# Attention weights turned on TensorE one block at a time, with another product between two of them

## The chip, the cores and the metric

The kernel runs on one core of a Trainium2 chip. The metric is the device time of one execution in microseconds (us), from the median of several runs. The engines of the core are TensorE (PE in the profile, and PEld for its loads of stationary operands), VectorE (DVE), ScalarE (ACT), GpSimd (POOL) and SyncE (SP, which issues most DMAs). Each takes its own instructions in the order in which the program wrote them.

## The reference

Two layers, each over 512 tokens of width 1024 in float32. Cut to what matters here:

```python
def hybrid_layer(x, w_in, w_out, ln_g, ln_b, rel_bias, topk):
    proj = jnp.einsum('bsd,dn->bsn', x, w_in)
    qA, kA, vA, gA, qB, kB, vB, gB, qI, kI, wI = jnp.split(proj, SPLIT_POINTS, axis=-1)
    oA = stick_breaking_attention(...)      # 8 heads of 64
    oB = dsa_sparse_attention(...)          # 8 heads of 64, top 128 keys of each query
    mix = jnp.concatenate([oA * jax.nn.silu(gA), oB * jax.nn.silu(gB)], axis=-1)
    y = jnp.einsum('bsm,md->bsd', mix, w_out)
    return layer_norm(ALPHA * x + y, ln_g, ln_b)
```

In the first group a weight is `sigmoid(z)` times the product of `1 - sigmoid` over the keys between it and the query. In the second group an indexer scores all keys, the best 128 of each query take part in a soft-max with a bias by distance, and the others are masked.

## The kernel before, in words

Every float32 operand of a product is held as a high and a low part (`XH` and `XL`, `whi` and `wlo`), and a product is three matmuls: high by high, low by high, high by low. A layer is a fixed list of 88 tasks. 24 are blocks of the indexer, then come 32 `Stick` tasks (8 heads of 4 blocks of 128 queries; block `qb` sees the first `qb + 1` blocks of keys), then 32 `Soft` tasks of the same shape. The loop over `s` in `layer` is the pipeline: in slot `s`, task `s` gets its logits `z` on PE (`stage0`: two matmuls of 128 to 512 columns), older tasks go through their later stages, and PE's remaining time in the slot is filled with matmuls of the big projections.

A `Soft` block goes like this. In slot `s` PE writes `z` (L518, L523); DVE subtracts the bias and finds the row's extreme (L762); ACT takes the exponential into `p` (L767). In the next slot, for the last head of a layer alone, ACT also scales `p` by the reciprocal of its sum (L777). In slot `s + 2` PE turns `p` around, block by block of 128 x 128 (`transpose`, L530, `qb + 1` transposes into the PSUM tile `tr`); ACT copies all of `tr` to the tile `AT` as its high part, one instruction (`evacuate`, L538), and DVE makes the low part from `tr` and the high part (`evacuate_lo`, L541). In slot `s + 3`, behind the last block of a head, PE multiplies `AT` with the values into `o`: eight matmuls at L701, the first with the high part, the second and third with the low part (`steps = [(1, 1), (2, 1), (1, 0), ...]`, where the second number is 1 for low). A `Stick` block runs the same way (transposes in slot `s + 3`, L727 and L730 in place of L538 and L541). Where a `Stick` head ends while a new one begins, the eight value matmuls are woven: one behind each of the first two `z` matmuls of 128 columns, the rest behind the transposes.

The fills are generators (`project_t`, `project_v`, `out_project`) that stand in one queue in a hand-written order; one step of a generator issues three matmuls (L266 to L268 of 512 columns into `pj`, L303 to L305 of 256 columns into `pjv`, L809 of 512 columns into `pjo`). `fill(t)` takes steps until the cost of the steps taken reaches the target at time `t` of a table of pins, and a slot calls it up to three times: ahead of the transposes, behind the low evacuation, and at its end. ACT, DVE and POOL take their instructions in the order of this loop: on ACT, for one, the evacuation of the older block stands ahead of the exponential of the new one (`stage1b`).

In the last four slots of a layer no `z` is left: PE has transposes of the last three blocks, six fill matmuls behind each run of transposes, the eight value matmuls of the last head, and then the output projection with nothing between (`pjo`, 90 matmuls in a row in the first layer, 162 in the second, by the chain of waits).

Of the kernel before, what the change touches and what calls it, by code (L numbers as in the profile page):

```python
# [17 lines left out]
P = 128  # L18
# [3 lines left out]
KC = D // P  # L22
# [80 lines left out]
def tile_hybrid(ctx: ExitStack, tc: tile.TileContext, xt, x, w_in, w_ki, w_out, ln_g, ln_b, rel_bias, onehot, out, depth=DEPTH):  # L103
# [154 lines left out]
    def run(gen):  # L258
# [2 lines left out]
            stream.prep_ahead()  # L261
        flush()

    def mm3(o, w, kc, first, last, tb):
        o = o.rearrange("p (a b) -> p a b", b=P)[:, tb:]
        T.matmul(o, w[0], XH[:, tb:, kc, :], start=first, stop=False)  # L266
        T.matmul(o, w[0], XL[:, tb:, kc, :], start=False, stop=False)  # L267
        T.matmul(o, w[1], XH[:, tb:, kc, :], start=False, stop=last)  # L268

    def first_block(unit):  # L270
        return 1 if unit[0] == "I" else 0
# [14 lines left out]
    def project_v(l, unit, vt, keys=None):  # L286
        i = index[l, unit]
        if keys is None:
            stream.prep(i + 1)
            w = [[t.rearrange("p (a b) -> p a b", b=W256) for t in stream.done[i + h]] for h in range(2)]  # L290
        else:
            stream.prep(i + 2)
            w = joined
        n = w[0][0].shape[2]
        vv = vt.rearrange("p t (h r) -> p t h r", r=P)
        for tb in range(NTB):
            if tb:
                stream.want = i + min(tb + 1, 3) + (keys is not None)
            full = ppj.tile([P, S], F32, tag="pj", name="pjv")[:, :n]
            acc = full[:, :W256]  # L300
            for kc in range(KC):
                whi, wlo = (t[:, kc % 4, :] for t in w[kc // 4])
                T.matmul(full, XH[:, tb, kc, :], whi, start=kc == 0, stop=False)  # L303
                T.matmul(full, XL[:, tb, kc, :], whi, start=False, stop=False)  # L304
                T.matmul(full, XH[:, tb, kc, :], wlo, start=False, stop=kc == KC - 1)  # L305
                if kc == KC - 1:
                    if keys is not None:
                        later.append(lambda tb=tb, full=full: keep_keys(tb, full))
                    if unit[0] == "A":
                        later.append(lambda tb=tb, acc=acc: A.activation(V_NOW[:, tb, :], acc, AF.Copy))  # L310
                    else:
                        later.append(lambda tb=tb, acc=acc: evac_v(vv, tb, acc))
                if (tb, kc) == (NTB - 1, KC - 1) and unit[0] == "A":
                    later.append(shift_values)
                    pending.append([SHIFT_SLOTS[1], lambda: value_steps(vv)])
                yield 324 * n // W256
# [193 lines left out]
    class Block:  # L510
# [13 lines left out]
            for head in weave:  # L524
                head.value(*head.steps.pop(0))

        def transpose(self):
            self.tr = ptr.tile([P, S], F32, tag="tr", name="tr")
            for sb in range(self.qb + 1):
                T.transpose(self.tr[:, sb * P : (sb + 1) * P], self.p[:, sb * P : (sb + 1) * P], ident)  # L530

        def blocks(self, t):
            b = t[:, self.qb * P : self.qb * P + P]
# [24 lines left out]
    def layer(l):  # L558
        last_layer = l == depth - 1
        st = {}  # L560
# [237 lines left out]
        def out_project(half, mts, tb, evac, acc=None, cols=slice(0, S), by_kind=False):  # L798
            if acc is None:
                acc = ppj.tile([P, S], F32, tag="pj", name="pjo")  # L800
            kinds = ((XH, 0), (XL, 0), (XH, 1))
            steps = [(m, k) for m in range(2 * mts[0], 2 * mts[-1] + 2) for k in kinds]
            if by_kind:
                early, all_ = range(2 * mts[0], 2 * mts[-1]), range(2 * mts[0], 2 * mts[-1] + 2)
                steps = [(m, k) for k, ms in ((0, early), (2, early), (0, all_[-2:]), (1, all_), (2, all_[-2:])) for m in ms]
                steps = [(m, kinds[k]) for m, k in steps]
            for n, (m, (mixed, part)) in enumerate(steps):
                w = stream.done[index[l, "o"] + 4 * half + m // 2][part][:, m % 2 * S : (m % 2 + 1) * S]
                T.matmul(acc[:, cols], mixed[:, tb, m, :], w[:, cols], start=n == 0, stop=n == len(steps) - 1)  # L809
                if n == len(steps) - 1:  # L810
                    later.append(lambda: evac(acc))
                if n % 3 == 2:
                    yield 648
# [13 lines left out]
        def target(s):  # L827
            for (a, ca), (b, cb) in zip(pins, pins[1:]):
                if s <= b:
                    return ca + (cb - ca) * max(0.0, (s - a) / max(b - a, 1e-9))  # L830
            return total

        st["done"] = 0
        st["gen"] = None

        def fill(s):
            while st["done"] < target(s) - 300:
                if st["gen"] is None:
                    if not queue:
                        return  # L840
                    st["gen"] = queue.pop(0)()
                step = next(st["gen"], None)
                if step is None:
                    st["gen"] = None
                else:
                    st["done"] += step

        rounds = [qb for _ in range(TOPK // 8) for qb in range(1, NTB)]

# [49 lines left out]
        for s in range(SLOTS + 3):  # L899
# [34 lines left out]
            if not sticks[0]:  # L934
                fill(now + FRAC[0])
            for old in olds:
                old.transpose()
                old.evacuate(old.head.at)
            if ended[0]:
                done.head.rest_of_values()  # L940
# [213 lines left out]
```

## Time and profile before

| what | value |
|---|---|
| median of 3 runs | 633.24 us (632.79 to 633.54) |
| the profiled execution's own time | 633.23 us |
| its span, first to last instruction | 631.4 us |
| PE busy | 622.5 us (99%), 3501 matmuls |
| DVE, ACT, POOL busy | 494.7, 343.6, 366.4 us |
| mean granted TensorE clock | 0.996 of full |
| transposes at L530 | 320: 160 of `om` (Stick), 160 of `p` (Soft) |

A matmul's record begins when PE starts to read for it and lasts until its result has landed, so neighbours overlap and a busy PE says little. What a matmul costs PE is the distance from its start to the next one's start. In a row of the time line, a row with "xN" holds N matmuls of one group that follow each other, and its duration runs from the first's start to the last's end. A number in front of a row is its start in us from the start of the span.

### The profile page before, as it was taken

The page shows a single profiled execution, that of the slowest core. Times are in us where ns is not written, and L with a number is a line of the kernel's source. Part 1 is how long each engine was busy: PE and PEld are TensorE (multiplying, and loading weights), DVE is VectorE, ACT ScalarE, POOL GpSimd, SP SyncE. Part 2 cuts the span into 40 slices and gives each one's busy share as a digit, 9 for nine tenths or more (in the row PEclk, how much of TensorE's full clock was granted, in tenths as well). Part 3 has the DMA queues.
Part 4 walks back from the last instruction along what each step waited for, and adds up shares of the span by engine and source line. Part 5 has one row for each costly group of instructions (what it writes and reads, how often), then busy time and mean ns, then how long its engine had stood idle before and what let it go on. Part 6 is the DMA issues. An engine that isn't in the chain of part 4 may idle for free.

```text
span 631.4 us, 10261 instructions
## 1 busy us (share of the span) xinstructions
PE 622.5 (99%) x3501; PEld 542.7 (86%) x3501; DVE 494.7 (78%) x1058; ACT 343.6 (54%) x686; POOL 366.4 (58%) x380
## 2 busy tenths in 40 slices
PE   9999999999999999999999999999999999999995
PEld 7988888988889889878899888899888898898784
DVE  3878999999975775668845789999999667656676
ACT  5686545454447566883135855554535566678700
POOL 5563544468465776898134544525756577778721
PEclk9999999999999999999999999999999999999998
DMA  7624243222362475453314242323123725644402
GB/s 239 215 78 133 101 133 102 82 86 68 98 174 80 133 187 168 124 191 118 134 68 133 103 133 100 114 87 125 43 101 90 194 86 140 171 131 142 166 34 100
DMA packets 31779, 77.41 MB, mean 123 GB/s; under 512 B 6572, under 2 KB 10668, under 8 KB 31728
## 3 DMA queue, kind: packets, MB, share of 16 engines
q1 hardware_dynamic: 31440, 76.51, 39.1%
q8 instruction: 27, 0.44, 0.3%
q10 hardware_dynamic: 288, 0.26, 0.1%
q14 instruction: 24, 0.20, 0.1%
HBM read 61.84 MB, written 4.44 MB: 105 GB/s over the span
## 4 chain that ended last, share of the span: by engine, by line
PE 91%; ACT 3%; POOL 2%; DMA 1%; DVE 1%; issue 1%; DVEq 0%; SPq 0%; POOLq 0%; ACTq 0%
PE pj L266 15%; PE pj L268 15%; PE pj L267 15%; PE pjo L809 11%; PE o L701 5%; PE tr L530 5%; PE z L523 4%; PE pjv L303 4%; PE pjv L304 4%; PE pjv L305 4%; PE z L518 4%; PE pjv L428 2%; PE pjq L430 1%; POOL wlo L215 1%; ACT p L767 1%; ACT p L777 1%
## 5 line engine op out<-in xcount | busy, mean ns | idle before, releaser
L215 POOL TENSOR_TENSOR wlo<-raw,whi 128x256 fp32r<-128x256 f32 (+1 forms) x250 | 230.9, 954 | 142.1 <-ACT whi L212 141.2
L266 PE MATMUL pj<-XH,whi 128*128 128x512 f32 (+1 forms) x432 | 171.6, 397 | 0.0
L268 PE MATMUL pj<-XH,wlo 128*128 128x512 f32 (+1 forms) x432 | 166.4, 385 | 0.0
L267 PE MATMUL pj<-XL,whi 128*128 128x512 f32 (+1 forms) x432 | 166.1, 385 | 0.0
L268 PEld LDWEIGHTS pj<-XH,wlo 128*128 128x128 f32 x432 | 81.1, 188 | 16.1
L266 PEld LDWEIGHTS pj<-XH,whi 128*128 128x128 f32 x432 | 81.2, 188 | 13.1
L717 ACT ACTIVATE om<-z 128x128 f32<-128x128 f32 (+1 forms) x64 | 28.1, 438 | 118.1 <-issue 68.4
L267 PEld LDWEIGHTS pj<-XL,whi 128*128 128x128 f32 x432 | 81.4, 188 | 12.4
L212 ACT ACTIVATE whi<-raw 128x1024 fp32r<-128x1024 f32 x78 | 82.0, 1056 | 2.5 <-DMA raw<-in_w_in_dram 1.9
L722 DVE TENSOR_TENSOR_SCAN om<-om,future 128x128 f32<-128x128 f32 (+1 forms) x64 | 67.6, 1056 | 0.2
L603 POOL TENSOR_TENSOR M<-M,mixt 64x512 f32<-64x512 f32 x24 | 33.9, 1413 | 51.0 <-DVE mixt L602 36.0
L303 PE MATMUL pjv<-whi,XH 128*128 128x256 f32 x192 | 56.8, 296 | 0.0
L305 PE MATMUL pjv<-wlo,XH 128*128 128x256 f32 x192 | 54.3, 283 | 0.0
L304 PE MATMUL pjv<-whi,XL 128*128 128x256 f32 x192 | 54.2, 282 | 0.0
L854 DVE MAX8 m<-scores 128x8 f32<-128x256 f32 (+2 forms) x96 | 52.9, 551 | 0.1
L855 DVE MATCH_REPLACE8 scores<-m,scores 128x256 f32<-128x256 f32 (+2 forms) x96 | 52.1, 543 | 0.0
L767 ACT ACTIVATE p<-p,mn 128x128 f32<-128x128 f32 (+1 forms) x64 | 35.8, 560 | 23.9 <-DVE mn L762 23.5
L701 PE MATMUL o<-AT,vt 128*128 128x512 f32 (+7 forms) x256 | 48.6, 316 | 0.0
L809 PE MATMUL pjo<-whi,XH 128*128 128x512 f32 (+1 forms) x118 | 41.2, 387 | 0.0
L809 PE MATMUL pjo<-wlo,XH 128*128 128x512 f32 (+1 forms) x118 | 41.0, 383 | 0.0
L523 PE MATMUL z<-k,q 128*128 128x128 f32 (+3 forms) x128 | 40.9, 320 | 0.0
L541 DVE TENSOR_TENSOR AT<-tr,AT 128x128 fp32r<-128x128 f32 (+1 forms) x64 | 31.2, 488 | 11.7 <-ACT AT L538 11.3
(165 smaller groups left out, 1290.8 us busy)
## 6 DMA issues: line engine op xcount, KB each, us to landing
raw<-in_w_in_dram SPq DMA_DIRECT2D x66, 512.0 KB, 3.4
k<-k SPq DMA_DIRECT2D x32, 256.0 KB, 5.1
raw<-in_w_out_dram SPq DMA_DIRECT2D x14, 512.0 KB, 3.2
gbias<-f_dram SPq DMA_DIRECT2D x18, 256.0 KB, 3.9
XN<-in_x_dram SPq DMA_DIRECT2D x8, 256.0 KB
y_dram<-XN SPq DMA_DIRECT2D x4, 512.0 KB, 2.6
XN<-y_dram SPq DMA_DIRECT2D x8, 256.0 KB, 3.9
M<-M SPq DMA_DIRECT2D x4, 448.0 KB
```

The lines of the kernel that those rows point to most:

```text
L212: A.activation(hi, src, AF.Copy)
L215: low = lambda lo=lo[:, c], src=src[:, c], hi=hi[:, c]: lo_engine.tensor_tensor(lo, src, hi, ALU.subtract)
L266: T.matmul(o, w[0], XH[:, tb:, kc, :], start=first, stop=False)
L267: T.matmul(o, w[0], XL[:, tb:, kc, :], start=False, stop=False)
L268: T.matmul(o, w[1], XH[:, tb:, kc, :], start=False, stop=last)
L303: T.matmul(full, XH[:, tb, kc, :], whi, start=kc == 0, stop=False)
L304: T.matmul(full, XL[:, tb, kc, :], whi, start=False, stop=False)
L305: T.matmul(full, XH[:, tb, kc, :], wlo, start=False, stop=kc == KC - 1)
L523: T.matmul(self.z[:, :nn], c, d, start=False, stop=True)
L701: T.matmul(self.o[:m, sb * P :], vt[:, sb, self.hh * P : self.hh * P + m], at_block(self.at[j], sb, sb, NTB - sb), start=(sb, j) == (0, 0) ...
L722: V.tensor_tensor_scan(rev, rev, future[:, S - n :][:, ::-1], 1.0, ALU.mult, ALU.max)
L809: T.matmul(acc[:, cols], mixed[:, tb, m, :], w[:, cols], start=n == 0, stop=n == len(steps) - 1)
```

## The change

`transpose` becomes `transposes`, which returns the single transposes as functions. In the slot loop the first of them is issued as before. For a `Soft` block the others go to a list, and steps of the fill queue are taken there and then; each fill matmul is issued through `fill_matmul`, which issues one waiting transpose behind it. So one fill matmul stands between two transposes. The steps count as done, and the later `fill` calls of the slot take as many fewer. For a `Stick` block whose slot also holds woven value matmuls, one value matmul goes between its two transposes; the other `Stick` blocks keep their transposes in one run. The evacuation is written behind the last transpose, as before.

```diff
+    between_fills = []
+
+    def fill_matmul(*args, **flags):
+        T.matmul(*args, **flags)
+        if between_fills:
+            between_fills.pop(0)()
...
-        T.matmul(o, w[0], XH[:, tb:, kc, :], start=first, stop=False)
+        fill_matmul(o, w[0], XH[:, tb:, kc, :], start=first, stop=False)
...
-        def transpose(self):
+        def transposes(self):
             self.tr = ptr.tile([P, S], F32, tag="tr", name="tr")
-            for sb in range(self.qb + 1):
-                T.transpose(self.tr[:, sb * P : (sb + 1) * P], self.p[:, sb * P : (sb + 1) * P], ident)
+            c = [slice(sb * P, (sb + 1) * P) for sb in range(self.qb + 1)]
+            return [lambda c=c: T.transpose(self.tr[:, c], self.p[:, c], ident) for c in c]
...
+        def next_fill():
+            if st["gen"] is None:
+                if not queue:
+                    return False
+                st["gen"] = queue.pop(0)()
+            step = next(st["gen"], None)
+            if step is None:
+                st["gen"] = None
+            else:
+                st["done"] += step
+            return True
+
         def fill(s):
-            while st["done"] < target(s) - 300:
...
+            while st["done"] < target(s) - 300 and next_fill():
+                pass
...
             for old in olds:
-                old.transpose()
+                first, *others = old.transposes()
+                first()
+                if old is softs[0]:
+                    between_fills.extend(others)
+                    while between_fills and next_fill():
+                        pass
+                    while between_fills:
+                        between_fills.pop(0)()
+                for t in others if old is sticks[0] else ():
+                    if ended[0]:
+                        done.head.value(*done.head.steps.pop(0))
+                    t()
                 old.evacuate(old.head.at)
```

The other fill matmuls (of `project_v` and `out_project`) go through `fill_matmul` in the same way. The instructions of ACT, DVE, POOL and SP stand in the same order before and after; only PE's order changes, and each slot holds the same matmuls as before. 110 of the 320 transposes get a matmul ahead of them in place of a transpose: 48 of `p` in each layer (18 behind 256-column fills, 30 behind 512-column ones) and 7 of `om` in each layer.

Three places show it. The first is on PE near the end of the first layer, in the slot that turns the last block (`qb` 3) of the last head but one: `z` is the newest block's logits, `tr<-ident,p` the transposes, `pjo` the fills of the output projection. Before:

```order
L518 MATMUL z<-k,q 128x256
L523 MATMUL z<-k,q 128x256
L530 MATMUL tr<-ident,p 128x128 x4
L809 MATMUL pjo<-whi_3012,XH 128x512
L809 MATMUL pjo<-whi_2815,XL 128x512 x2
L809 MATMUL pjo<-whi_2891,XL 128x512 x2
L809 MATMUL pjo<-whi_3012,XL 128x512
L518 MATMUL z<-k,q 128x384
```

And now:

```order
L525 MATMUL z<-k,q 128x256
L530 MATMUL z<-k,q 128x256
L537 MATMUL tr<-ident,p 128x128
L267 MATMUL pjo<-whi_3012,XH 128x512
L537 MATMUL tr<-ident,p 128x128
L267 MATMUL pjo<-whi_2815,XL 128x512
L537 MATMUL tr<-ident,p 128x128
L267 MATMUL pjo<-whi_2815,XL 128x512
L537 MATMUL tr<-ident,p 128x128
L267 MATMUL pjo<-whi_2891,XL 128x512 x2
L267 MATMUL pjo<-whi_3012,XL 128x512
L525 MATMUL z<-k,q 128x384
```

The first transpose stands where it stood; the fourth has moved behind three fill matmuls that used to follow it.

The second place is PE at the end of the layer, where the last block of the last head is turned and its values follow (`o<-AT_107` reads the high part, `o<-AT_108` the low part). Before:

```order
L809 MATMUL pjo<-whi_2815,XL 128x512 x2
L530 MATMUL tr<-ident,p 128x128 x4
L809 MATMUL pjo<-whi_2891,XL 128x512 x2
L809 MATMUL pjo<-whi_3012,XL 128x512 x2
L809 MATMUL pjo<-wlo_3013,XH 128x512 x2
L701 MATMUL o<-AT_107,vt 128x512
L701 MATMUL o<-AT_108,vt 64x384
```

And now:

```order
L267 MATMUL pjo<-whi_2815,XL 128x512 x2
L537 MATMUL tr<-ident,p 128x128
L267 MATMUL pjo<-whi_2891,XL 128x512
L537 MATMUL tr<-ident,p 128x128
L267 MATMUL pjo<-whi_2891,XL 128x512
L537 MATMUL tr<-ident,p 128x128
L267 MATMUL pjo<-whi_3012,XL 128x512
L537 MATMUL tr<-ident,p 128x128
L267 MATMUL pjo<-whi_3012,XL 128x512
L267 MATMUL pjo<-wlo_3013,XH 128x512 x2
L708 MATMUL o<-AT_107,vt 128x512
L708 MATMUL o<-AT_108,vt 64x384
```

Between the last transpose and the first value matmul stood six fill matmuls; now three stand there.

The third place is a woven `Stick` run on PE in the first layer (`tr<-ident,om`). Before:

```order
L523 MATMUL z<-k,q 128x128
L701 MATMUL o<-AT_106,vt 64x256
L530 MATMUL tr<-ident,om 128x128 x2
L701 MATMUL o<-AT_105,vt 128x384
L701 MATMUL o<-AT_105,vt 128x256
```

And now:

```order
L530 MATMUL z<-k,q 128x128
L708 MATMUL o<-AT_106,vt 64x256
L537 MATMUL tr<-ident,om 128x128
L708 MATMUL o<-AT_105,vt 128x384
L537 MATMUL tr<-ident,om 128x128
L708 MATMUL o<-AT_105,vt 128x256
```

The second transpose has moved behind the value matmul of 384 columns.

More of the change, by code (lines that the diff above doesn't have):

```diff
@@ L262, in run @@
         flush()
+    between_fills = []
[3 more added lines that the diff above has]
+            between_fills.pop(0)()
     def mm3(o, w, kc, first, last, tb):
         o = o.rearrange("p (a b) -> p a b", b=P)[:, tb:]
-        T.matmul(o, w[0], XH[:, tb:, kc, :], start=first, stop=False)
-        T.matmul(o, w[0], XL[:, tb:, kc, :], start=False, stop=False)
-        T.matmul(o, w[1], XH[:, tb:, kc, :], start=False, stop=last)
+        fill_matmul(o, w[0], XH[:, tb:, kc, :], start=first, stop=False)
+        fill_matmul(o, w[0], XL[:, tb:, kc, :], start=False, stop=False)
+        fill_matmul(o, w[1], XH[:, tb:, kc, :], start=False, stop=last)
     def first_block(unit):
@@ L302, in project_v @@
                 whi, wlo = (t[:, kc % 4, :] for t in w[kc // 4])
-                T.matmul(full, XH[:, tb, kc, :], whi, start=kc == 0, stop=False)
-                T.matmul(full, XL[:, tb, kc, :], whi, start=False, stop=False)
-                T.matmul(full, XH[:, tb, kc, :], wlo, start=False, stop=kc == KC - 1)
+                fill_matmul(full, XH[:, tb, kc, :], whi, start=kc == 0, stop=False)
+                fill_matmul(full, XL[:, tb, kc, :], whi, start=False, stop=False)
+                fill_matmul(full, XH[:, tb, kc, :], wlo, start=False, stop=kc == KC - 1)
                 if kc == KC - 1:
@@ L808, in out_project @@
                 w = stream.done[index[l, "o"] + 4 * half + m // 2][part][:, m % 2 * S : (m % 2 + 1) * S]
-                T.matmul(acc[:, cols], mixed[:, tb, m, :], w[:, cols], start=n == 0, stop=n == len(steps) - 1)
+                fill_matmul(acc[:, cols], mixed[:, tb, m, :], w[:, cols], start=n == 0, stop=n == len(steps) - 1)
                 if n == len(steps) - 1:
@@ L834, in layer @@
         st["gen"] = None
-        def fill(s):
-            while st["done"] < target(s) - 300:
[L838 to L846, printed above, removed]
+        def next_fill():
[9 more added lines that the diff above has]
+            return True
+        def fill(s):
+            while st["done"] < target(s) - 300 and next_fill():
+                pass
         rounds = [qb for _ in range(TOPK // 8) for qb in range(1, NTB)]
```

## The prediction

> **What bounds the kernel now.** The page comes first: the span, PE's share of it, and the chain of work that ended last.
>
> ```profile
> span 631.4 us, 10261 instructions
> ...
> PE 91%; ACT 3%; POOL 2%; DMA 1%; DVE 1%; issue 1%; DVEq 0%; SPq 0%; POOLq 0%; ACTq 0%
> ```
>
> PE is the bound over nine tenths of the span. So a nanosecond per transpose on PE counts in full there, and the rest is decided by where PE waits. The waits of PE's loads say that it hardly does in the attention part:
>
> ```profile
> PEld tr L530 <- ACT p L777: 1.5, 4, 0.6
> ...
> PEld o L701 <- DVE AT L541: 1.0, 4, 0.3
> ```
>
> Columns: total us, times, longest. Four times a transpose waits for the scaled `p` of a layer's last head, four times a value matmul waits for the low part of `AT`. The chain, asked for its end of the first layer, shows what leads to the first of these (start, us, what):
>
> ```profile
> 270.86 0.50 ACT p L767 x2
> 271.36 0.48 ACT AT L538
> 271.84 0.29 ACT p L777
> 272.13 0.49 ACT p L767 x2
> ...
> 277.99 0.73 ACT p L777
> 278.73 0.04 issue
> 278.77 0.66 PE tr L530 x4
> 279.43 1.38 PE pjo L809 x6
> 280.81 1.18 PE o L701 x8
> ```
>
> And the window view has ACT's busy time (fourth engine) in the 7.4 us between, here and at the same place of the second layer:
>
> ```profile
> 271.30:278.70 7.40, 7.40 (x39) 5.61 (x37) 4.59 (x16) 7.12 (x18) 6.45 (x6) 1.00 0.56 178
> 581.80:589.20 7.40, 7.37 (x39) 5.47 (x37) 4.62 (x16) 7.12 (x18) 6.37 (x6) 1.00 0.55 186
> ```
>
> ACT works 7.12 of 7.40 us, in program order, from an `AT` evacuation to the `p` that the last run of transposes waits for. From there to the end of the layer PE has no idle time (the last three rows of the chain, then 90 output matmuls). So at two places per layer something that ACT or DVE does late makes PE late, and the change moves work towards both.
>
> **The price of a transpose on PE.** Two stretches of PE's time line, among 512-column fills, first a run of four, then a transpose that stands singly already before the change (blocks with `qb` 0 have one):
>
> ```profile
> 221.31 0.39 PE L268 MATMUL pj<-XH,wlo 128*128 128x512 f32 x1
> 221.54 0.60 PE L530 MATMUL tr<-ident,p 128*128 128x128 f32 x4
> 221.90 0.48 PE L266 MATMUL pj<-XH,whi 128*128 128x512 f32 x1
> 222.21 0.40 PE L267 MATMUL pj<-XL,whi 128*128 128x512 f32 x1
> ...
> 225.11 0.27 PE L530 MATMUL tr<-ident,p 128*128 128x128 f32 x1
> 225.14 0.47 PE L266 MATMUL pj<-XH,whi 128*128 128x512 f32 x1
> 225.45 0.39 PE L267 MATMUL pj<-XL,whi 128*128 128x512 f32 x1
> ```
>
> A 512-column matmul holds PE for 0.23 us (221.31 to 221.54). The run, with the one fill behind it, takes 222.21 - 221.54 = 0.67 us; less the fill's 0.23 that is 0.44 for four, 0.11 each. The single transpose with its fill takes 225.45 - 225.11 = 0.34 us, less 0.23: 0.11 again. The fill behind a transpose starts 0.03 after it but then runs 0.08 longer (0.47 against 0.39), so nothing is hidden; it is only booked elsewhere. The single one is exactly what the change makes of the others: a 512-column fill, a transpose, a 512-column fill. The same among 256-column fills:
>
> ```profile
> 246.02 0.60 PE L530 MATMUL tr<-ident,p 128*128 128x128 f32 x4
> 246.37 0.36 PE L303 MATMUL pjv<-whi,XH 128*128 128x256 f32 x1
> 246.57 0.28 PE L304 MATMUL pjv<-whi,XL 128*128 128x256 f32 x1
> 246.69 0.28 PE L305 MATMUL pjv<-wlo,XH 128*128 128x256 f32 x1
> ...
> 248.24 0.27 PE L530 MATMUL tr<-ident,p 128*128 128x128 f32 x1
> 248.27 0.36 PE L303 MATMUL pjv<-whi,XH 128*128 128x256 f32 x1
> 248.47 0.28 PE L304 MATMUL pjv<-whi,XL 128*128 128x256 f32 x1
> ```
>
> Here a fill is 0.12 (246.57 to 246.69). Four in a run: 0.55 - 0.12 = 0.43, 0.11 each. One alone: 0.23 - 0.12 = 0.11. For the 110 transposes that the change separates PE pays the same, within what two decimals can show: between 0 and 0.01 us more each, 0 to 1.1 us in all. I take 0.3, near the lower end, since the rows agree. The 14 woven `Stick` transposes are among the 110; the value matmul that goes between has the same load of 128 columns behind a transpose as the fills have, so I price it alike.
>
> The Trainium skill, in "TensorE: Matmul & The Clock Gate", section "LDWEIGHTS (loading the stationary operand)", gives a load of 128 columns about 128 / 1.2 = 107 ns, and in "Part 2: What happens when you issue a matmul" it says that a load is pulled ahead under the matmul that is running. By that a run of transposes goes at the pace of loads, which the trace bears out (0.11 each), and a transpose between two wide fills has its own load hidden, which speaks for this change. But by the same rule the next fill's load then has only the transpose to hide under, and comes into the open instead; the row at 225.11 (0.11 us for a lone transpose) agrees with that second half.
>
> **What comes later.** ACT's evacuation of `tr` waits for the last transpose of its run. In a run the fourth starts 0.33 us after the first (221.90 - 0.03 - 221.54). With fills between, each step is 0.34 (225.11 to 225.45), so it starts 1.02 after: 0.69 us later, while the first stands where it did. Among 256-column fills the step is 0.23 and the shift 0.36. For most of the 48 slots per kernel with such runs this costs nothing: the `AT` blocks are read a slot later, and the new block's exponential, behind the evacuation on ACT, is needed two slots later, each slot being 2 to 4 us. `p`, `tr` and `z` have room for that: PE shows no wait there now. I price these at zero; at the worst a slip of one `p` by 0.24 us (a run of three among 256-column fills, 2 x (0.23 - 0.11)) runs through POOL's weight splits into PE in the first layer.
>
> Two places per layer have no such cover. The first is the evacuation of the last block of the last head but one. PE's run and ACT's instruction, in the first and the second layer:
>
> ```profile
> 270.42 0.60 PE L530 MATMUL tr<-ident,p 128*128 128x128 f32 x4
> 271.27 0.57 ACT L538 ACTIVATE AT<-tr 128x512 fp32r<-128x512 f32 x1
> ...
> 580.81 0.60 PE L530 MATMUL tr<-ident,p 128*128 128x128 f32 x4
> 581.79 0.58 ACT L538 ACTIVATE AT<-tr 128x512 fp32r<-128x512 f32 x1
> ```
>
> Before, the run ends at 271.02 and the evacuation starts at 271.27, behind an exponential. After, it ends at 271.02 + 0.69 = 271.71 and the evacuation starts 0.04 later (by the row at 279.46 below, 0.03 after the run's end at 279.43): at 271.75, 0.48 later. From here ACT is full, so the scaled `p` that the last run waits for at 278.77 comes 0.48 later too. PE's fills in this stretch can't help: PE waits there already. In the second layer the same gives 580.81 + 0.60 + 0.69 + 0.04 = 582.14 against 581.79: 0.35. Together **0.83 us**; the bounds are 0, if ACT has slack that its rows hide (7.40 - 7.12 = 0.28 per layer is the most that shows), and 0.48 in each.
>
> The second place is the last run of all, with its evacuation, its low part on DVE and the values:
>
> ```profile
> 279.46 0.60 ACT L538 ACTIVATE AT<-tr 128x512 fp32r<-128x512 f32 x1 [0.37 <-PE tr L530]
> ...
> 280.10 0.69 DVE L541 TENSOR_TENSOR AT<-tr,AT 128x512 fp32r<-128x512 f32 x1 [0.41 <-ACT AT L538]
> ...
> 280.65 1.34 PE L701 MATMUL o<-AT,vt 128*128 128x512 f32 x8
> ...
> 590.62 0.69 DVE L541 TENSOR_TENSOR AT<-tr,AT 128x512 fp32r<-128x512 f32 x1 [0.41 <-ACT AT L538]
> ...
> 591.17 1.35 PE L701 MATMUL o<-AT,vt 128*128 128x512 f32 x8
> ```
>
> Before, the run begins at 278.77 and ends at 279.43; ACT is done at 280.06, DVE at 280.79. PE reaches the first value matmul at 280.65 and the second, which reads the low part, at 280.88: 0.09 to spare. After, the run ends 0.69 later, so DVE is done at 281.48. PE, whose six fills and four transposes are the same, still reaches the second value matmul at 280.88 and now waits; with the 0.05 that its load needs behind the wait, it starts at 281.53, 0.65 later. Queued behind it are the other six value matmuls and the whole output projection, and nothing on PE takes it up. The second layer ends the same way (the low part done at 591.31, the second value matmul at 591.40: the same 0.09). Together **1.30 us**; the bounds are 0 and 2 x 0.75.
>
> The sum: 0.3 + 0.83 + 1.30 = 2.4 us on the profiled execution's 633.23, whose span is 631.4 and which agrees with the median, 633.24. That makes **635.7 us**, 0.4% slower. About 0.2% (1.27 us) is what a measurement of this kernel can tell from no change.
>
> **The rivals.** *Faster: the loads are hidden after all.* The mechanism is the first half of the rule cited above: alone between wide fills a transpose costs only its streaming. The nearest row is a 128-column matmul in the woven part:
>
> ```profile
> 111.49 0.22 PE L518 MATMUL z<-k,q 128*128 128x128 f32 x1
> 111.55 0.34 PE L701 MATMUL o<-AT,vt 128*64 128x384 f32 x1
> ```
>
> It holds PE for 0.06 us, so 0.05 less than a transpose. 110 x 0.05 = 5.5 us saved, less up to the 2.1 us of the two late places: 629.8. It decides as soon as a lone transpose costs under 0.09 us. Against it stand the lone transposes in the trace, at 0.11 among both kinds of fill, and that the matmul at 111.55 has a stationary operand of 64 columns, which the fills have not. I give it 0.08.
>
> *No change: the late evacuations are covered.* ACT makes up the 0.83 in gaps or in an order of events that the profile hides, or the values find their low part in time. With one of the two gone the time is 634.4 or 634.8, with both 633.5. Against it: DVE's 0.69 and ACT's 0.60 are in series with the run, and ACT's gaps in the window are 0.28. For a result within 0.2% I give 0.20.
>
> *Slower still.* The lone transposes cost the full 0.01 more each (+0.8 over what I took), and the 0.24 us slip of the first layer arrives: 636.7 to 637.0. It is inside the forecast's side; I count it with it, at 0.72 in all.
>
> *The change does nothing* can be left out: the order shows no run of `p` transposes left.
>
> **How the numbers follow.** The likeliest is the forecast, 635.7. The range goes down through the covered cases to 633.3 (only the 0 to 0.3 us on PE) and up to 637.0 (all upper bounds); left out are the faster rival's 0.08 and a tenth for what I have not seen. Faster by over 0.2%: 0.08; within: 0.20; slower by over 0.2%: 0.72.
>
> **What would show it.** Right: a transpose with the fill behind it still takes 0.34 us among 512-column fills and 0.23 among 256-column ones; the evacuation that now starts at 271.27 starts about 0.5 us later against the run's first transpose, and the last run with it; the second value matmul of a layer's last head starts about 0.9 us after the first, in place of 0.23, and PE's loads at L701 wait for DVE some 1.3 us more in total. Wrong: a transpose and its fill in 0.30 us or less, a stretch between 200 and 255 us that is shorter than before, or a last run of transposes that begins no later than before.

## The result, and the profile after

The kernel with the change takes 637.19 us (median of 6 executions, 636.82 to 637.60); the kernel before takes 633.39 us (6 executions, 632.79 to 634.21). The ratio is 1.0057, with a 95% interval of 1.0048 to 1.0067: 3.8 us slower. The direction was forecast, the size was not: 635.7 was the number and 637.0 the end of the range.

The page of the changed kernel, its span and the chain of waits:

```profile
span 635.5 us, 10261 instructions
...
PE 94%; ACT 3%; DVE 1%; DMA 1%; issue 0%; SPq 0%; POOL 0%; DVEq 0%; POOLq 0%; ACTq 0%
```

PE carries even more of the chain than before (94% against 91%). That doesn't say that PE has more work. The waits of its loads (total us, times, longest) say that it waits longer:

```profile
PEld tr L537 <- ACT p L784: 2.3, 4, 0.6
PEld o L708 <- DVE AT L548: 1.7, 4, 0.5
...
PEld tr L537 <- ACT p L774: 0.9, 2, 0.5
PEld o L708 <- ACT AT L545: 0.9, 2, 0.4
```

L537, L784, L708 and L548 are the former L530, L777, L701 and L541; L774 and L545 are the former L767 and L538. The first wait was 1.5 us and the second 1.0 us before. The third was 0.5, with 0.2 at the longest; the fourth is new among the ten longest. The prediction had asked for some 1.3 us more of the second wait. It is 0.7 more, because the fourth now stands ahead of it: the first value matmul already waits, for ACT's high part.

The single transposes, on PE's time line, among 512-column fills and among 256-column fills:

```profile
222.53 0.27 PE L537 MATMUL tr<-ident,p 128*128 128x128 f32 x1
222.56 0.48 PE L267 MATMUL pj<-XL,whi 128*128 128x512 f32 x1
222.88 0.27 PE L537 MATMUL tr<-ident,p 128*128 128x128 f32 x1
...
246.97 0.27 PE L537 MATMUL tr<-ident,p 128*128 128x128 f32 x1
247.00 0.37 PE L267 MATMUL pjv<-whi,XL 128*128 128x256 f32 x1
247.20 0.27 PE L537 MATMUL tr<-ident,p 128*128 128x128 f32 x1
```

From transpose to transpose it is 0.35 and 0.23 us with one fill between: 0.34 and 0.23 had been forecast. To within 0.01 us the separated transposes of `p` cost what they cost in a run.

Next the two late places. ACT's evacuation of the last block of the last head but one, and ACT's busy time (fourth engine) from there to the end of the scaled `p` that the last run needs, in both layers:

```profile
272.85 0.60 ACT L545 ACTIVATE AT<-tr 128x512 fp32r<-128x512 f32 x1 [0.51 <-PE tr L537]
...
585.14 0.60 ACT L545 ACTIVATE AT<-tr 128x512 fp32r<-128x512 f32 x1 [0.46 <-PE tr L537]
```

```profile
272.88:280.32 7.44, 7.21 (x37) 5.10 (x35) 4.12 (x13) 7.16 (x17) 5.94 (x6) 1.00 0.57 196
585.17:592.60 7.43, 7.21 (x37) 5.09 (x35) 4.12 (x13) 7.15 (x17) 5.92 (x6) 1.00 0.64 195
```

ACT now waits for PE's transposes 0.51 and 0.46 us, where it came behind an exponential before. Then it is as full as it was: 7.16 of 7.44 us, against 7.12 of 7.40 before. And the end of the layer:

```profile
280.37 0.33 PE L537 MATMUL tr<-ident,p 128*128 128x128 f32 x1
...
282.43 0.50 PE L708 MATMUL o<-AT,vt 128*128 128x512 f32 x1
283.15 1.16 PE L708 MATMUL o<-AT,vt 128*64 128x384 f32 x7 [0.23 <-DVE AT L548]
```

The second value matmul starts 0.72 us after the first, in place of 0.23 (280.65 to 280.88 before). The first one is late as well: ACT's copy was done 0.59 us before PE came to it (280.06 and 280.65 before), and the run, counted from its own start, now ends 0.71 later (280.37 to 281.74, against 278.77 to 279.43).

Set against the profiled execution of before, PE's landmarks (the starts of the same matmuls) are late by this much, per stretch of the program:

| stretch | first layer | second layer | in the prediction |
|---|---|---|---|
| up to the first `z` | 0.39 | | not in it |
| `Stick` part, with the woven slots | 0.27 | 0.27 | in the 0.3 for the pace |
| `Soft` heads up to the sixth | 0.07 | 0.07 | in the 0.3 for the pace |
| the sixth head's run of four | 0.26 | 0.23 | the slip, priced at zero |
| the sixth head's values | 0.09 | 0.06 | not in it |
| from there to the last run | 0.07 | 0.08 | 0.03 in the 0.3 for the pace; 0.045 at the seventh head's values, not in it |
| the last run's first transpose | 0.45 | 0.31 | 0.83 together |
| from the last run through the values | 0.74 | 0.73 | 1.30 together |

The sum is the 4.09 us by which the spans differ (635.491 - 631.406). The 0.39 ahead of the first `z` is not the change's: PE's order there is the same in both kernels, and this stretch also differs between executions of kernels that are alike there, by -0.09 to +0.53 us against before in nine profiles of the experiments, by 1.05 and 2.27 in two. Without it 3.7 us are left, close to the 3.8 us between the medians. The 0.045 at the seventh head's values is one step: the second of the eight matmuls takes 0.216 us instead of 0.171, in both layers, and 0.170 and 0.176 in the experiment below that keeps that head's last run whole. So it belongs to a late evacuation, not to the pace.

### The profile page after: what moved, and what is told of

It is laid out like the page before. It is cut to its first block, busy times and chain, and to the rows that moved or that the text cites. A ratio compares the mean times of both kernels' runs of the same rounds, so it can differ in the third digit from the quotient of the medians.

```text
span 635.5 us, 10261 instructions
## 1 busy us (share of the span) xinstructions
PE 625.2 (98%) x3501; PEld 541.3 (85%) x3501; DVE 495.3 (78%) x1058; ACT 343.9 (54%) x686; POOL 365.8 (58%) x380
## 4 chain that ended last, share of the span: by engine, by line
PE 94%; ACT 3%; DVE 1%; DMA 1%; issue 0%; SPq 0%; POOL 0%; DVEq 0%; POOLq 0%; ACTq 0%
PE pj L267 46%; PE pjv L267 13%; PE pjo L267 12%; PE o L708 6%; PE tr L537 5%; PE z L530 4%; PE z L525 4%; PE pjv L435 2%; PE pjq L437 1%; ACT p L774 1%; ACT AT L545 1%; ACT p L784 1%; ACT whi L212 1%; DMA q_raw<-in_w_in_dram 1%; PE trx L1094 1%; ACT mixt L607 0%
## 5 line engine op out<-in xcount | busy, mean ns | idle before, releaser
L212 ACT ACTIVATE whi<-raw 128x1024 fp32r<-128x1024 f32 x78 | 82.0, 1056 | 2.2 <-DMA raw<-in_w_in_dram 1.7
L267 PE MATMUL pjv<-whi,XL 128*128 128x256 f32 x192 | 55.7, 290 | 0.0
L708 PE MATMUL o<-AT,vt 128*128 128x512 f32 (+7 forms) x256 | 49.3, 322 | 0.5 <-DVE AT L548 0.5
L774 ACT ACTIVATE p<-p,mn 128x128 f32<-128x128 f32 (+1 forms) x64 | 35.8, 559 | 20.6 <-DVE mn L769 19.8
L548 DVE TENSOR_TENSOR AT<-tr,AT 128x128 fp32r<-128x128 f32 (+1 forms) x64 | 31.2, 488 | 17.7 <-ACT AT L545 17.3
L537 PE MATMUL tr<-ident,p 128*128 128x128 f32 x160 | 42.5, 275 | 1.1 <-ACT p L774 0.5
```

Of the source, the lines that this page charges most:

```text
L212: A.activation(hi, src, AF.Copy)
L267: T.matmul(*args, **flags)
L537: return [lambda c=c: T.transpose(self.tr[:, c], self.p[:, c], ident) for c in c]
L548: V.tensor_tensor(self.blocks(at[1]), self.src, self.blocks(at[0]), ALU.subtract)
L708: T.matmul(self.o[:m, sb * P :], vt[:, sb, self.hh * P : self.hh * P + m], at_block(self.at[j], sb, sb, NTB - sb), start=(sb, j) == (0, 0) ...
L774: A.activation(p, p, AF.Exp, bias=h.mn[:, b], scale=-1.0, accum_out=h.sums[:, b])
```

## The experiments

Two theories stood against each other. **L (late evacuations):** a single transpose costs as much as one in a run; the time comes from evacuations that start later, at few places, where PE, ACT or DVE have no cover. **P (price):** each separated transpose costs PE some 0.035 us more, 3.8 us over 110. Unless a diff says otherwise, an edit is to the changed kernel, and the choice of runs to separate was made by one condition:

```diff
-                if old is softs[0]:
+                apart = old is softs[0] and (CONDITION)
+                if apart:
                     between_fills.extend(others)
...
-                for t in others if old is sticks[0] else ():
-                    if ended[0]:
+                for t in () if apart else others:
+                    if ended[0] and old is sticks[0]:
```

Where the text says that only some `Soft` runs are separated, the `Stick` runs stay whole too: there the two lines with `ended[0]` and the value matmul are left out. In the conditions a `Soft` block is a pair of its head (0 to 7, in the order in which they are worked on) and its `qb`. "Head 5" in the code is the sixth head in the text.

**Only the woven `Stick` runs.** CONDITION is `False`: the `Soft` runs stay whole.

> Of the change only the woven Stick runs (14 transposes with a value matmul between); the Soft runs stand as before. Theory L (a transpose costs PE the same alone or in a run, and the loss is in late evacuations of the last three heads): the trace of the changed kernel gains 0.07 us per woven slot, 14 x 0.07 = 1.0 less what runs back, which it shows as 0.26 per layer, so +0.5 us; no wait at the end of a layer beyond those of before. Theory P (each separated transpose costs PE some 0.035 us more, 3.8 us over 110): 14 x 0.035 = +0.5 us, and a longer distance from transpose to transpose in the woven rows. The total is the same by both; the rows tell: by L the distances around the transposes sum to what they did and the fills behind are slower.

Measured: 633.76 us against 633.34, ratio 1.0006 (0.9998 to 1.0015), 0.4 us slower, though the interval still holds zero. The trace places it. PE's time line behind a woven slot, the kernel before first, then this one (the first fill behind the slot, and the `z` behind twelve fills):

```profile
142.74 0.39 PE L266 MATMUL pj<-XH,whi 128*128 128x512 f32 x1
...
145.46 0.28 PE L518 MATMUL z<-k,q 128*128 128x256 f32 x1
```

```profile
142.87 0.39 PE L267 MATMUL pj<-XH,whi 128*128 128x512 f32 x1
...
145.63 0.28 PE L525 MATMUL z<-k,q 128*128 128x256 f32 x1
```

Twelve fills took 2.72 us before and take 2.76 now; the woven slot itself is longer by 0.03. In four of the seven woven slots of a layer the sum is 0.07 us, in the other three between 0 and -0.02 us, in both layers and to within 0.002 us the same in this kernel and in the full change. So the woven part costs 0.27 us a layer, and most of it lies in the fills that follow. Why a fill of 512 columns takes 0.224 to 0.236 us there instead of 0.227 is open. (One of the three slots without loss had such fills already before the change.)

**Only the first three `Soft` heads.** CONDITION is head < 3: 36 of the 110 transposes are separated, and no late place is touched.

> Of the change only the Soft runs of the first three of eight heads (18 transposes per layer, 36 in all), everything else as before. L: these lie among plenty of fills, so only the pace counts: 24 among 512-column fills at 0.006 and 12 among 256-column ones at 0.002, +0.2 us, within 0.4 of before. P: 36 x 0.035 = +1.3 us.

Measured: 633.43 against 633.34, ratio 1.0000 (0.9992 to 1.0009). P asked for 1.3 us and falls: 36 separated transposes cost nothing that the times can show. In the trace they cost 0.06 us a layer.

**The change without two runs per layer.** CONDITION is all but heads 6 and 7 with `qb` 3: 12 of the 110 transposes go back into runs of four.

> The change, but with two runs of four per layer kept whole: the last block of the last head but one and of the last head (12 of the 110 transposes stay in runs). L: the steps of 0.44 and 0.30 us at the last head's transposes and of 0.71 us at its values in each layer go, 2.2 us in all, so +1.6 us against before and 2.2 under the change. P: 98 of 110 remain, +3.4 us.

Measured: 634.57 against 633.34, ratio 1.0019 (1.0010 to 1.0028), 1.2 us slower than before and 2.6 us faster than the change. 12 transposes carry 2.6 of 3.8 us; by P they would carry 0.4, by L 2.2. The waits of PE's loads in this kernel:

```profile
PEld o L708 <- DVE AT L548: 1.1, 4, 0.3
...
PEld tr L537 <- ACT p L774: 0.9, 2, 0.5
```

The wait for DVE's low part is back at before's level (1.0). The wait for the exponential (L774, 0.9, 0.5 at the longest) is not: that one belongs to another run.

**A narrow load behind the transpose.** The prediction had explained the price of 0.11 us with the next matmul's load of 128 columns. Here the woven `Stick` values come in an order in which the matmul behind a transpose has a stationary operand of 64 columns; the `Soft` runs stay whole.

```diff
                 self.steps = [(1, 1), (2, 1), (1, 0), (2, 0), (3, 0), (3, 1), (0, 1)]
+                if self.kind == "A":
+                    self.steps = [(1, 0), (2, 0), (1, 1), (2, 1), (3, 0), (3, 1), (0, 1)]
```

> The woven part alone again, with the order of a Stick head's value matmuls changed so that the ones with a stationary operand of 64 columns stand behind the two transposes, and those of 128 columns behind the two 128-column z matmuls. If a lone transpose costs 0.11 us because the next matmul's load of 128 columns then comes into the open, it costs about 0.06 here, and the z matmuls, 0.06 before, cost 0.11; total as with the woven part alone within 0.3 us. If the 0.11 is the transpose's own streaming, it stays 0.11 and the time rises by 28 x 0.05 = 1.4 us over the woven part alone.

Measured: 634.95 against 633.34, ratio 1.0025 (1.0016 to 1.0035), 1.2 us more than with the first order. PE's time line in a woven slot, of the first experiment and then of this one (128*64 is a stationary operand of 64 columns):

```profile
111.62 0.22 PE L525 MATMUL z<-k,q 128*128 128x128 f32 x1
111.68 0.34 PE L708 MATMUL o<-AT,vt 128*64 128x384 f32 x1
111.86 0.22 PE L530 MATMUL z<-k,q 128*128 128x128 f32 x1
...
112.04 0.27 PE L537 MATMUL tr<-ident,om 128*128 128x128 f32 x1
112.07 0.43 PE L708 MATMUL o<-AT,vt 128*128 128x384 f32 x1
112.33 0.27 PE L537 MATMUL tr<-ident,om 128*128 128x128 f32 x1
```

```profile
111.54 0.22 PE L525 MATMUL z<-k,q 128*128 128x128 f32 x1
111.60 0.39 PE L710 MATMUL o<-AT,vt 128*128 128x384 f32 x1
111.83 0.22 PE L530 MATMUL z<-k,q 128*128 128x128 f32 x1
...
112.06 0.27 PE L537 MATMUL tr<-ident,om 128*128 128x128 f32 x1
112.09 0.42 PE L710 MATMUL o<-AT,vt 128*64 128x384 f32 x1
112.35 0.27 PE L537 MATMUL tr<-ident,om 128*128 128x128 f32 x1
```

From transpose to transpose it is 0.29 us with either load behind: 0.17 for a 384-column matmul, 0.11 to 0.12 for the transpose. So the width of the next load does not set the transpose's price. An ordinary 128-column matmul does depend on it: `z` with the 384-column matmul behind it takes 0.24 us with a 64-column load next (111.62 to 111.86) and 0.29 with one of 128 columns (111.54 to 111.83). Less 0.17 to 0.18, that is 0.06 and 0.11 to 0.12. The 0.05 at two places per woven slot, 14 slots in all, is 1.4 us, about the 1.2 us measured.

**Only one run of three.** CONDITION is head 3 with `qb` 2, two transposes per layer. Its evacuation comes 0.24 us later. The prediction followed that slip and priced it at zero.

> Of the change one run of three per layer: the third block of the fourth Soft head, among 256-column fills (2 transposes per layer, 4 in all). L: its evacuation on ACT ends 0.24 us later, and the weight split behind it, POOL's low parts, the gate products and the split of the mix carry that on to the scaled and unscaled exponentials 18 us later, so PE's first transpose of the sixth head's last run (at 262.47 before) and of the layer's last run (at 278.77) come 0.24 later: +0.5 us in both layers together. If the slip is absorbed on the way, nothing. P: 4 x 0.035 = +0.14 us.

Measured: 633.99 against 633.34, ratio 1.0011 (1.0002 to 1.0020), 0.65 us slower. The interval, 0.1 to 1.3 us, does not exclude P's 0.14; the trace decides. 18 us behind the separated run, PE waits at the sixth head's run of four, which is whole in this kernel:

```profile
262.85 0.66 PE L537 MATMUL tr<-ident,p 128*128 128x128 f32 x4 [0.28 <-ACT p L774]
```

PE's start there is 0.26 us late beyond before's own wait (0.435 against 0.176 us over the usual pace), and the second layer shows the same. The links between can be followed in the profiles of before and of the change, by starts: the evacuation of the run of three 244.55 and 245.51 (PE is 0.72 late here, so 0.24 more), the weights' high part on ACT (L212) 245.33 and 246.29, their low part on POOL 246.45 and 247.41, behind it POOL's bias product for a new block (L753) 248.93 and 249.90, DVE's row extreme that waits for it 249.89 and 250.87, ACT's exponential 250.55 and 251.53 and its `mixt` 251.29 and 252.26, then by way of DVE back to POOL, whose product into `M` starts at 256.62 and 257.60, `XH` on ACT 257.94 and 258.93. The last two links stand in ACT's time line, of before and of the change:

```profile
257.94 0.85 ACT L166 ACTIVATE XH<-M 128x768 fp32r<-128x768 f32 x1 [0.24 <-POOL M L691]
...
261.60 0.72 ACT L767 ACTIVATE p<-p,mn 128x512 f32<-128x512 f32 x1
```

```profile
258.93 0.84 ACT L166 ACTIVATE XH<-M 128x768 fp32r<-128x768 f32 x1 [0.50 <-POOL M L698]
...
262.58 0.72 ACT L774 ACTIVATE p<-p,mn 128x512 f32<-128x512 f32 x1
```

ACT waits for POOL, and the exponential `p` arrives 0.98 us later while PE is only 0.73 late. The slip has travelled the whole way undiminished. (The trace of the single run of three is longer by more than the two slips: in its first layer ACT waits 1.45 us for the weight transfer that it splits into `wo`, 1.06 before, and PE is another 0.37 late by the last run. That wait is 1.37 in the next experiment, where this run is whole, so it need not be the slip's.)

**Only the last run of all.** CONDITION is head 7 with `qb` 3, three transposes per layer.

> Of the change only the last run of four of a layer (6 transposes in all). L: no transposes start later before it, so its first one stands where it stood, and the values behind it wait for ACT and DVE: 0.71 us per layer, +1.4 us. P: 6 x 0.035 = +0.2 us.

Measured: 635.06 against 633.34, ratio 1.0024 (1.0014 to 1.0033), 1.7 us slower with six separated transposes. PE's time line at the end of the first layer:

```profile
281.27 0.49 PE L708 MATMUL o<-AT,vt 128*128 128x512 f32 x1
281.99 1.16 PE L708 MATMUL o<-AT,vt 128*64 128x384 f32 x7 [0.23 <-DVE AT L548]
```

0.72 us from the first to the second value matmul, as in the full change: 0.49 over the usual pace, and the first one is 0.17 late behind ACT's high part, with 0.04 more behind the wait. Together 0.7 a layer, 1.4 us of the 1.7; the rest is within the interval. (The profiled execution lost more elsewhere: in its second layer ACT waits 1.88 us for a weight transfer into `raw`, 1.23 before.)

**The low parts later in the values' order.** In the full change, the `Soft` values take three more high-part terms ahead of the low parts.

```diff
+                if self.kind == "B":
+                    self.steps = [(1, 0), (2, 0), (3, 0), (1, 1), (2, 1), (3, 1), (0, 1)]
```

> The change, with the values of a Soft head in another order: the two matmuls that read the low part of all keys stand behind the four of the high part, so the low part is needed 0.35 us later (one of 384, one of 256, one of 128 columns). L: the wait for DVE at the second value matmul shrinks from 0.50 to 0.15 at the end of a layer, and the one of 0.19 (with 0.05 behind it) at the sixth head goes: 1.0 to 1.2 us less than the change, +2.7 us against before. P: the order of the values changes nothing, +3.8 us.

Measured: 636.31 us, 3.0 us above before (ratio 1.0045, 1.0032 to 1.0058) where the change was 3.8 above its own. The two intervals overlap, so the times alone don't show the gain of 0.8 us; the traces, from the first `z` to the end, have the same 0.8. Through the last head's values PE now loses 0.18 us a layer in place of 0.54, so most of that wait was path time. Part is given back: at the fifth head's values the term `(3, 0)` now stands where the fourth block of the values isn't ready yet, and the eight matmuls take 1.63 us instead of 1.41.

**Relief for ACT, without the change.** If ACT's evacuations are what is late, taking work from ACT should make the kernel before faster. The last head's scaling of `p` was moved to DVE, with the value order of the experiment above.

```diff
-                A.activation(p, p, AF.Copy, scale=h.rec[:, b])
+                V.tensor_scalar(p, p, h.rec[:, b], None, ALU.mult)
```

> The kernel before, with two relaxations at the places that the change made worse: the Soft value order with the low part last, and the scaling of the last head's p by the reciprocal of its sums on DVE in place of ACT (four instructions per layer, 2.2 us of ACT). L: PE's wait of 0.24 plus 0.06 at the layer's last transposes and of 0.13 plus 0.05 at the sixth head's values go, 0.5 us per layer: -0.9 us against before. P says nothing of it: 0.

Measured: 645.29 against 633.34, ratio 1.0194 (1.0171 to 1.0216), 12 us slower: the expectation failed. DVE's time line, then POOL's:

```profile
278.98 3.88 DVE L779 TENSOR_SCALAR p<-p,rec 128x384 f32<-128x384 f32 x1
```

```profile
278.94 1.26 POOL L603 TENSOR_TENSOR M<-M,mixt 64x512 f32<-64x512 f32 x1 [0.98 <-DVE rec L778]
280.16 2.48 POOL L215 TENSOR_TENSOR wlo<-raw,whi 128x512 fp32r<-128x512 f32 x2
```

The scaling takes 3.88 us; it ends at 282.86, just behind POOL's three instructions (282.64). PE's transposes wait 8.7 us in all for such scalings. Its form of 512 columns took 0.49 us where POOL was idle. The Trainium skill, in "SBUF — State Buffer", section "Who interferes with whom", says that DVE and GpSimd share a pair of ports as an exclusive lock, that `tensor_scalar` can take it, that the one that comes second is blocked, and that the form that also writes out its accumulator does not take it. The rows agree with the blocking: POOL began first, at 278.94.

**The same relief in the other form.** The accumulator form, on the kernel before, with the value order `(1, 0), (2, 0), (1, 1), (2, 1), (3, 0), (3, 1), (0, 1)`.

```diff
+                self.spare = over_sum[0][:, NTB : NTB + 1]
...
-                A.activation(p, p, AF.Copy, scale=h.rec[:, b])
+                V.tensor_scalar(p, p, h.rec[:, b], 0.0, ALU.mult, ALU.add, accum_out=h.spare)
```

> The kernel before, with the scaling of the last head's p again on DVE in place of ACT, but in a form that also sums its result into a spare column (two instructions), and with the low parts of a Soft head's values behind the high parts of 512, 384 and 256 columns. If the run with the plain form on DVE lost its 6 us per layer because that form cannot run while POOL works, and this form can, then PE's waits of 0.24 + 0.06 us at the layer's last transposes and 0.13 + 0.05 us at the sixth head's values go: -0.9 us against before. If DVE was simply too full for the extra work, it loses again, by several us.

Measured: 635.12 against 633.42, ratio 1.0022 (1.0012 to 1.0031), 1.7 us slower (the ratio leaves out one of its eleven executions, of 3549.92 us). DVE, then ACT:

```profile
276.42 0.61 DVE L780 TENSOR_SCALAR_CACHE_REDUCE p<-p,rec 128x384 f32<-128x384 f32 x1
...
276.95 0.69 DVE L765 CUSTOM_DVE_ANT_0 p<-z,XN 128x512 f32<-128x512 f32 x1
```

```profile
277.74 0.72 ACT L770 ACTIVATE p<-p,mn 128x512 f32<-128x512 f32 x1 [0.80 <-DVE mn L765]
```

Here 384 columns take 0.61 us while POOL works: this form is not blocked, as that section of the Trainium skill has it. But the scaling stands ahead of the row extreme on DVE, the exponential waits 0.80 us for that, and PE's wait at the last run grows from 0.24 to 0.77 us. The relief has moved the bound of this stretch from ACT to DVE. In its second layer the profiled execution also loses 0.7 us where ACT waits 1.88 us for a weight transfer, as in the experiment on the last run, so the 1.7 us are not all the scaling's.

**The value order alone, on the kernel before.**

```diff
+                if self.kind == "B":
+                    self.steps = [(1, 0), (2, 0), (1, 1), (2, 1), (3, 0), (3, 1), (0, 1)]
```

> The kernel before with one line changed: the Soft values' product takes the low parts of the weights behind the two high-part terms of the first blocks, in the order (1,0), (2,0), (1,1), (2,1), (3,0), (3,1), (0,1). Theory L (TensorE's short waits for the last evacuations are whole path time): the wait for the low part at the sixth head's values, 0.13 us in each Soft layer, and some 0.05 us at the last run's values go, so 0.36 us less than before, 633.0 where before is 633.4. Rival (such waits only move to the next operand): 0, 633.4.

Measured: 633.55 against 633.45, ratio 1.0001 (0.9992 to 1.0010). The interval holds both L's 0.36 less and the rival's 0, so the times don't decide; the trace speaks for the rival, waits that only move. PE's landmarks in the first layer show the gain and its loss: 0.17 us saved at the sixth head's values, and by the last run 0.37 lost again. ACT's split of `wo`, of before and of this kernel:

```profile
268.07 1.06 ACT L212 ACTIVATE wo<-raw 128x1024 fp32r<-128x1024 f32 x1 [1.06 <-DMA raw<-in_w_out_dram]
```

```profile
268.67 1.06 ACT L212 ACTIVATE wo<-raw 128x1024 fp32r<-128x1024 f32 x1 [1.26 <-DMA raw<-in_w_out_dram]
```

And the wait of this kernel's PE loads for the scaled `p`, which was 1.5 us before:

```profile
PEld tr L530 <- ACT p L779: 1.9, 4, 0.6
```

ACT's row starts 0.60 later, of which 0.42 was there at the first `z`; the other 0.18 is in the transfer itself, from issue to ACT's start 3.49 us in place of 3.31. ACT waits for this transfer, whose issue waits for POOL to be done with the buffer, and not for the sixth head's values on PE. ACT's next evacuations, exponentials and scalings, up to the last run's `p`, are late by the same 0.59 to 0.60. So PE was done with these values sooner, and from there on waited the longer for ACT: by the saved 0.17, and by the slower transfer. That reading is from one trace; the transfer's part in it was not tried by itself.

**A fill ahead of two whole runs.** The kernel before, the same value order, and one fill matmul moved ahead of the runs of four of heads 5 and 7 (`fill_matmul` issues the whole run behind the next fill).

```diff
+                run_of = old.transposes()
+                if old is softs[0] and (2 * old.head.pair + old.head.s - 8, old.qb) in ((5, 3), (7, 3)):
+                    between_fills.append(lambda: [t() for t in run_of])
+                    next_fill()
+                else:
+                    for t in run_of:
+                        t()
```

> The kernel before, all runs of transposes whole, with the value order of e10 and one fill matmul moved ahead of the run of four of the sixth head's and of the last head's last pair step, where TensorE waits 0.18 and 0.24 us for the scaled block and 0.06 us more. Theory L: the fill covers the wait, the run starts no later than it did, so besides the 0.36 us of the order another 0.8 us or so is saved over two layers: 1.2 us less than before (0.8 to 1.4), 632.2 where before is 633.4. Rival P (the price is in the separated transposes) and the rival that waits only move: what e10 gives and no more, 0 to -0.36.

Measured: 632.95 against 633.45, ratio 0.9992 (0.9983 to 1.0001): 0.5 us less than before, half of what L asked for, and the interval just includes no change. In its trace the stretch from the first `z` to the end is 0.50 us shorter than before's. PE's time line at the last run:

```profile
278.98 0.86 PE L267 MATMUL pjo<-whi,XL 128*128 128x512 f32 x3
279.74 0.66 PE L537 MATMUL tr<-ident,p 128*128 128x128 f32 x4
280.15 0.93 PE L267 MATMUL pjo<-whi,XL 128*128 128x512 f32 x3
280.92 0.62 PE L267 MATMUL pjo<-wlo,XH 128*128 128x512 f32 x2
281.38 0.86 PE L710 MATMUL o<-AT,vt 128*128 128x512 f32 x4
```

Five fills in place of six behind the run, and the values start 1.64 us after its first transpose instead of 1.88: 0.23 saved in each layer. By the end of the sixth head's values 0.31 and 0.33 are saved as well, but 0.23 and 0.39 come back as waits further on, ahead of the last run. It is the fastest version here; that it is faster than the kernel before is likely, not shown.

## Why the prediction was right in direction and short in size

*The price of a transpose on PE, 0.3 us: right for `Soft`, too low for the woven runs.* The `Soft` part pays some 0.1 us a layer, 0.2 in all, and 36 separated transposes alone cost nothing that the times can show. The sentence that failed is "so I price it alike": the 14 woven transposes cost 0.54 us, the larger part in the fills behind them, which the rows at 111 us could not show. The bound of 1.1 us held the sum of both (0.74).

*The reason for that price: wrong.* The prediction took the lone transpose's 0.11 us for the next load coming into the open. It leaned on the formula that the Trainium skill gives in "TensorE: Matmul & The Clock Gate", section "LDWEIGHTS (loading the stationary operand)": columns divided by 1.2, in ns, which makes an estimate of 107 ns for a load of 128 columns. With a 64-column load behind it, the transpose still takes 0.11 to 0.12. In this kernel the price belongs to the transpose, and the forecast of 0.34 and 0.23 us held because it came from rows, not because of that reason. The load's width does set the price of the ordinary 128-column matmul, 0.06 or 0.11 us. That also settles the rival of hidden loads: its row at 111.49 was no transpose.

*"I price these at zero": the failed step.* The slip of 0.24 us through POOL arrived in full, and in both layers rather than the first: 0.26 and 0.23 at the sixth head's run of four, and one run of three alone costs 0.65 us (0.1 to 1.3 by its interval). The reason given was that PE shows no wait there. But PE did show one in the kernel before, small and not among the rows of the prediction:

```profile
PEld tr L530 <- ACT p L767: 0.5, 2, 0.2
```

A run of transposes that already waits has nothing to take up a slip of the block that it waits for. At the same place another 0.09 and 0.06 us went at the values, where a low part was already late, and 0.045 in each layer at the seventh head's.

*The evacuation of the last head but one, 0.83: right.* 0.45 and 0.31 measured, 0.76 together, against 0.48 and 0.35.

*The last run and its values, 1.30: right in kind, a little short.* 0.74 and 0.73 us measured. The prediction let only the low part on DVE be late (0.65). The high part on ACT is late too, by 0.18, and behind the second wait another 0.04 goes, at the third value matmul. The run alone, with nothing else of the change, shows the same rows.

The sum: 2.4 us forecast, 3.7 found in the traces. The difference of 1.3 is made of the slip (0.5), the woven runs with the pace (0.74 in place of 0.3), the values of the sixth and the seventh head (0.24) and the end of the layer (0.17), less 0.07 at the evacuation of the last head but one. What happened is close to the rival called "slower still", with the slip twice instead of once. The range ended at that rival's 637.0, with the slip in one layer only; the time lies 0.19 above, and before itself was 0.15 higher in this comparison than the 633.24 from which I counted.

## What to carry to other kernels

Splitting a run of small matmuls with wide ones cost the engine next to nothing by itself here, though among narrow ones it cost half a microsecond. What it does is to move the end of the run, and whoever waits for the whole run pays. Ask for each run who reads its last part and which engine has no gap from there to the next wait of the bound, and follow a slip through every engine, since one of a quarter microsecond went through ACT, POOL and DVE and came out 18 us later undiminished. A short wait of the busiest engine need not be worth its length: where the late engine has a bound of its own further up, the wait can just move, as the trace with the other value order suggests.

## What the runs showed of the hardware

A float32 transpose of 128 x 128 cost PE 0.11 to 0.12 us in a run, alone among wide fills, and alone with a 64-column or a 128-column load behind it. A 128-column matmul cost 0.06 or 0.11 us by the width of the next load. Behind some slots of narrow matmuls, nine or so fills of 512 columns took 0.224 to 0.236 us instead of 0.227, in nearly the same sequence each time; before, one woven slot of a layer had this, with the change five. The cause is open. A DVE multiplication of `p` by a scalar took 3.88 us while POOL worked (128x384), and 0.61 us for the same size beside POOL in the form with an accumulator.
